# The second half of x loaded in 32-wide blocks and turned on VectorE; the third z group turned in the last block

## The chip, the cores and the metric

The kernel runs on one core of a Trainium2 chip. The metric is device time in microseconds (us) of one execution. The core has TensorE (matrix products into PSUM), VectorE (DVE in the profile), ScalarE (ACT), GpSimd (POOL) and SyncE (SP). SP, ScalarE and GpSimd can issue DMAs, each in the order of its own queue; all of them run on the core's 16 DMA engines.

## The reference

One inference step of a decoder layer with width 2048, for 256 prompt tokens and 32 sample tokens (8 sequences of 4), 288 tokens in all:

```
x = x + 1/2 * post1(SwiGLU_1(pre1(x)))      # RMSNorm before and after; inner width 5632
x = x + post2(HybridMixer(pre2(x)))         # GLA heads and HGRN2 heads, two recurrences
x = x + 1/2 * post3(SwiGLU_2(pre3(x)))

swiglu(x) = (silu(x @ w_gate) * (x @ w_up)) @ w_out
rmsnorm(x, g) = x * rsqrt(mean(x * x) + 1e-6) * g
```

The outputs are x for the prompt and for the sample tokens and the new states of the recurrences. Everything is 32-bit floating point, and the layer's weights, about 360 MB, are read once from HBM.

## The kernel before

**Layout.** x is held feature-major: 16 tiles x[k] of 128 features by 288 tokens. In DRAM it is token-major, so each tile has to be turned on the way in, and the result turned back on the way out.

**Products in three parts.** To keep 32-bit precision each operand is split into a rounded high part and the rest. For x, `split_x` (or `split_to`, lines 251 to 257) makes xh on ScalarE (line 252, with the norm's gain) and then xl on VectorE (line 253), which needs xh. For the weights, `Weights.pieces` makes wh on ScalarE (line 95) and wl on VectorE (line 96). Each product is three matmuls: xh by wh, xl by wh, xh by wl (lines 520 to 522). The rows' factor from the norm (rt) is multiplied in after the product, so that the products of the first block can begin before the norm is known.

**Weights.** A unit is 512 KB: 1024 columns by 128 partitions, in the FFN two steps k of 512 columns. SP issues the loads (line 63; the first unit as two rows, line 72) into three buffers named raw; `W.ahead` splits units into four buffers of wh and wl. A unit's load waits until the split has freed its raw buffer.

**Blocks.** `block` (line 511) multiplies 16 tiles of x by a column block of 512, into four PSUM tiles f. In the order of the program step k does its 12 matmuls (four f by three parts); after each step the block's `tick(k)` is called. The last `tail` units are done f by f, each f followed by its evacuation `evac`; then the ticks of those steps. The first FFN is `gate_0`, `up_0`, then pairs of these with `out` blocks of the chunk before. The framework's scheduler takes the program's order as its priority and sets each engine's order by its own estimates; `tc.issue_after(i)` keeps what is inside it behind instruction i in that order. Engines wait for each other by semaphores only where data or a buffer asks for it.

**The start.** `load_x(j)` loads two tiles of x token-major (128 tokens by 256 features, and 32 sample tokens) on SP (lines 276 and 277), after a memset of the rest of the third part. Eight such buffers are held. `x_tile(k)` turns one tile: three TensorE transposes by the identity into PSUM (lines 305 and 306), the split from PSUM, and a copy to x[k], on ScalarE for odd k (line 310) and on VectorE for even k (line 312). `x_first` is called by the first block's tick (`PreNorm.tick0`), two tiles ahead: after step k for tile k + 2. The first two tiles are made before the block; warm-up matmuls (line 294) stand around them. GpSimd issues four small parameter loads into stage2 (lines 265 to 268), ScalarE the load of the gains (line 264) and of araw, 2048 pieces of 64 B of the mixer's weights (line 775).

**The end.** In the last `out` blocks, out2_9_0 to out2_9_3 with two chunks each, every evacuated tile y[k] is squared and summed, and ScalarE makes z = y times gain (line 680). The tiles of the first three blocks (o < 3) are turned back in blocks of 32 by 32 on VectorE (`turn32`, lines 625 and 627, into one buffer b32 and bs32), and after the fourth tile `move32` (lines 636 and 640) moves the 32-blocks to their places in zT and zS, 20 DMAs that alternate between GpSimd's and SP's queues. The last block's four tiles are transposed on TensorE. `finish` then computes the norm, adds z and x (line 725) by quarters s = 0 to 3 and stores.

Of the kernel before, what the change touches and what calls it, by code (L numbers as in the profile page):

```python
# [16 lines left out]
P = 128  # L17
# [107 lines left out]
def trunk_kernel(ctx, tc, x_prompt, x_sample, state_gla, state_hgrn, norm_gains, f1_in, f1_out, f2_in, f2_out,  # L125
# [109 lines left out]

    FIRST = 2
    AHEAD = 4
    UPDATED = 8
# [17 lines left out]
    def split_x(gi, k):  # L256
        return split_to((xh[k], xl[k]), x[k], gain(gi, k))

    first = ExitStack()
    ldp = first.enter_context(tc.tile_pool(name="ld", bufs=8, side="right"))  # L260
    stage = ldp.tile([96, P], F32, name="stage", bufs=1)
    stage2 = ldp.tile([P, P], F32, name="stage2", bufs=1)
    G.memset(stage2, 0.0)
    S.dma_start(stage, norm_gains.rearrange("o g (k p) -> (o g k) p", p=P))
    G.dma_start(stage2[0:4, :], gla_b.rearrange("o (k p) -> (o k) p", p=P))
    G.dma_start(stage2[4:12, :], hgrn_gamma.rearrange("o (k p) -> (o k) p", p=P))
    G.dma_start(stage2[12:14, :], gla_norm.rearrange("o (k p) -> (o k) p", p=P))
    G.dma_start(stage2[14:15, :], hgrn_norm)
    xins = []
# [18 lines left out]
    load_x(3)  # L288
    load_x(4)
    def warm(n):  # L290
# [8 lines left out]
    V.tensor_copy(prm[:, 0:96], tp[:, 0:96])  # L299

    def x_tile(k):
        xin, c = xins[k // 2], slice(k % 2 * P, (k % 2 + 1) * P)
        tp = auxtile(f"tp_x{k}")
        for t in range(2):
            PE.transpose(tp[:, t * P:(t + 1) * P], xin[:, t, c], ident)
        PE.transpose(tp[:, TP:TP + P], xin[:, 2, c], ident)
        ins = split_to((xh[k], xl[k]), tp[:, 0:T], gain(0, k))
        with tc.issue_after(ins[0]), tc.issue_after(ins[1]):
            if k % 2:
                S.activation(x[k], tp[:, 0:T], AF.Copy)  # L310
            else:
                V.tensor_copy(x[k], tp[:, 0:T])
        return ins

    unit = []

    def x_first(k):

        with tc.issue_after(product[0]) if k >= FIRST else ExitStack():
            ins = x_tile(k)  # L320
        if k < 4:
            if k % 2 == 0:
                unit.append(W.pieces(2))
            with tc.issue_after(ins[0]), tc.issue_after(ins[1]):
                ins = next(unit[-1])
        if k % 2 == 1:
            if k >= 3:
                with tc.issue_after(ins[0]), tc.issue_after(ins[1]):
                    W.ahead(1)
            W.fill()  # L330
            if k // 2 + 5 < KT // 2:
                load_x(k // 2 + 5)
        return ins
# [232 lines left out]
    def ffn(tag, gcol, gnext, pn, before, fill=None):  # L566
# [3 lines left out]
        with ExitStack() as pools:  # L570
# [42 lines left out]

            lasts, zs = [], []

# [40 lines left out]
            def do_out(c, n):  # L656
# [8 lines left out]
                for o in range(4):  # L665
                    def ev(f, ps):
# [5 lines left out]
                        if end:  # L672
# [18 lines left out]
                    k = 4 * (c - 4) + o  # L691
# [49 lines left out]
    def mixer(pn, border):  # L741
        with ExitStack() as mx:
# [687 lines left out]

    pn = PreNorm("pre1", x_first, FIRST, 11)
    pn.late.append(prm2)
# [44 lines left out]
```

## Time and profile before

| what | value |
|---|---|
| median of 3 runs | 2281.41 us (2281.22 to 2283.21) |
| profiled execution, its own time | 2280.79 us |
| its span in the profile | 2279.0 us |
| TensorE matmuls busy | 2264.1 us, 99% |
| VectorE, ScalarE, GpSimd busy | 62%, 45%, 5% |
| granted TensorE clock, mean | 0.999 |
| DMA | 382 MB, mean 168 GB/s |

How to read the lines shown below. A line of the timeline has the start in us from the start of the span, the duration in us, engine, source line, operation, output and input tiles, their shapes, how many instructions were merged, and in brackets how long the engine was idle before it and what released it. A line of a group has the number of instructions, busy time in us, mean time of one in ns, and idle time before them by releaser; where it gives three durations they are the least, the median and the greatest, in ns. SPq is SP's queue of DMA issues. In the DMA view q1 holds SP's transfers, q10 ScalarE's and q0 GpSimd's: packets, MB, and the time their packets took as a share of the 16 engines' time; its GB/s row gives 40 equal slices of the stretch asked for. Matmul durations in the rows overlap, as TensorE is pipelined: the distance from start to start is the pace.

### The profile page before, as it was taken

The page shows a single profiled execution, that of the slowest core. Times are in us where ns is not written, and L with a number is a line of the kernel's source. Part 1 is how long each engine was busy: PE and PEld are TensorE (multiplying, and loading weights), DVE is VectorE, ACT ScalarE, POOL GpSimd, SP SyncE. Part 2 cuts the span into 40 slices and gives each one's busy share as a digit, 9 for nine tenths or more (in the row PEclk, how much of TensorE's full clock was granted, in tenths as well). Part 3 has the DMA queues.
Part 4 walks back from the last instruction along what each step waited for, and adds up shares of the span by engine and source line. Part 5 has one row for each costly group of instructions (what it writes and reads, how often), then busy time and mean ns, then how long its engine had stood idle before and what let it go on. Part 6 is the DMA issues. An engine that isn't in the chain of part 4 may idle for free.

```text
span 2279.0 us, 42090 instructions
## 1 busy us (share of the span) xinstructions
PE 2264.1 (99%) x17164; PEld 2252.0 (99%) x17164; DVE 1420.8 (62%) x2375; ACT 1034.4 (45%) x1603; POOL 115.8 (5%) x204
## 2 busy tenths in 40 slices
PE   9999999999999999999999999999999999999998
PEld 9999999999999999999999999999999999999997
DVE  7545545554555468889889754954555455545546
ACT  6443333333334346556656654644333333333344
POOL 0000000000000002001000000260000000000003
PEclk9999999999999999999999999999999999999999
DMA  7555555555555545456465554475555555555555
GB/s 218 169 165 165 165 167 165 166 166 167 167 167 185 166 158 163 139 171 198 144 183 159 167 183 160 141 203 169 165 166 164 166 167 166 167 167 167 167 163 151
DMA packets 228801, 382.42 MB, mean 168 GB/s; under 512 B 24018, under 2 KB 63936, under 8 KB 228608
## 3 DMA queue, kind: packets, MB, share of 16 engines
q1 hardware_dynamic: 219088, 366.27, 50.7%
q0 software_dynamic: 7344, 13.29, 2.1%
q8 instruction: 134, 2.20, 0.4%
q10 hardware_dynamic: 2176, 0.18, 0.1%
q14 instruction: 59, 0.48, 0.1%
HBM read 363.75 MB, written 11.80 MB: 165 GB/s over the span
## 4 chain that ended last, share of the span: by engine, by line
PE 94%; DVE 3%; DMA 1%; ACT 1%; issue 0%; DVEq 0%; SPq 0%; ACTq 0%
PE gate L522 9%; PE gate L520 9%; PE gate L521 9%; PE up L522 8%; PE up L520 8%; PE up L521 8%; PE out L521 8%; PE out L522 8%; PE out L520 8%; PE hfq L520 2%; PE hfq L522 2%; PE mo L522 1%; PE mo L520 1%; PE mo L521 1%; PE hfq L521 1%; PE v L520 1%
## 5 line engine op out<-in xcount | busy, mean ns | idle before, releaser
L96 DVE TENSOR_TENSOR wl<-raw,wh 128x1024 fp32r<-128x1024 f32 (+1 forms) x674 | 821.6, 1219 | 621.0 <-ACT wh L95 619.1
L95 ACT ACTIVATE wh<-raw 128x1024 fp32r<-128x1024 f32 (+1 forms) x674 | 711.6, 1057 | 1017.6 <-PE gate L521 315.8
L522 PE MATMUL gate<-xh,wl 128*128 128x288 f32 x1660 | 489.0, 295 | 0.2 <-DVE wl L96 0.2
L520 PE MATMUL gate<-xh,wh 128*128 128x288 f32 x1660 | 488.9, 296 | 0.3 <-ACT wh L95 0.3
L521 PE MATMUL gate<-xl,wh 128*128 128x288 f32 x1660 | 485.5, 295 | 0.0
L522 PE MATMUL out<-hh,wl 128*128 128x288 f32 x1408 | 415.1, 295 | 0.9 <-DVE wl L96 0.9
L521 PE MATMUL out<-hl,wh 128*128 128x288 f32 x1408 | 415.7, 295 | 0.0
L522 PE MATMUL up<-xh,wl 128*128 128x288 f32 x1408 | 415.0, 295 | 0.0
L520 PE MATMUL up<-xh,wh 128*128 128x288 f32 x1408 | 414.8, 295 | 0.1
L521 PE MATMUL up<-xl,wh 128*128 128x288 f32 x1408 | 414.6, 294 | 0.0
L520 PE MATMUL out<-hh,wh 128*128 128x288 f32 x1408 | 413.7, 294 | 0.0
L522 PEld LDWEIGHTS gate<-xh,wl 128*128 128x128 f32 x1660 | 311.5, 188 | 0.6 <-DVE wl L96 0.6
L520 PEld LDWEIGHTS gate<-xh,wh 128*128 128x128 f32 x1660 | 310.9, 188 | 1.2 <-ACT wh L95 0.5
L521 PEld LDWEIGHTS gate<-xl,wh 128*128 128x128 f32 x1660 | 310.4, 188 | 0.2
L522 PEld LDWEIGHTS out<-hh,wl 128*128 128x128 f32 x1408 | 264.7, 188 | 1.1 <-DVE wl L96 1.1
L520 PEld LDWEIGHTS out<-hh,wh 128*128 128x128 f32 x1408 | 264.6, 188 | 0.0
L520 PEld LDWEIGHTS up<-xh,wh 128*128 128x128 f32 x1408 | 264.1, 188 | 0.5 <-ACT g L590 0.3
L521 PEld LDWEIGHTS out<-hl,wh 128*128 128x128 f32 x1408 | 264.4, 188 | 0.0
L521 PEld LDWEIGHTS up<-xl,wh 128*128 128x128 f32 x1408 | 264.2, 188 | 0.1
L522 PEld LDWEIGHTS up<-xh,wl 128*128 128x128 f32 x1408 | 264.2, 188 | 0.0
L671 DVE TENSOR_TENSOR y<-out,y 128x288 f32<-128x288 f32 x288 | 121.4, 452 | 98.9 <-PE out L522 95.9
L520 PE MATMUL hfq<-xh,wh 128*128 128x288 f32 x256 | 77.5, 303 | 0.0
(381 smaller groups left out, 2598.2 us busy)
## 6 DMA issues: line engine op xcount, KB each, us to landing
raw<-in_ffn_w_in_dram SPq DMA_DIRECT2D x351, 512.0 KB, 3.4
raw<-in_ffn_w_out_dram SPq DMA_DIRECT2D x176, 512.0 KB, 3.5
raw<-in_mix_w_in_dram SPq DMA_DIRECT2D x64, 512.0 KB, 3.7
raw<-in_mix_w_in_dram SPq DMA_DIRECT2D x96, 256.0 KB, 3.2
raw<-in_mix_w_out_dram SPq DMA_DIRECT2D x32, 512.0 KB, 3.7
out_dram<-s POOLq DMA_DIRECT2D x32, 256.0 KB, 3.5
s<-in_state_gla_dram SPq DMA_DIRECT2D x16, 256.0 KB, 4.2
s<-in_state_hgrn_dram SPq DMA_DIRECT2D x16, 256.0 KB, 3.6
```

The source lines that it names most:

```text
L95: i1 = self.nc.scalar.activation(h[:, c], raw[:, c], AF.Copy).ins
L96: i2 = self.nc.vector.tensor_tensor(l[:, c], raw[:, c], h[:, c].bitcast(F32), op=ALU.subtract).ins
L520: yield lambda: PE.matmul(dst, w[0][:, c:c + P], parts[0], start=start, stop=False)
L521: yield lambda: PE.matmul(dst, w[0][:, c:c + P], parts[1], start=False, stop=False)
L522: yield lambda: PE.matmul(dst, w[1][:, c:c + P], parts[0], start=False, stop=stop)
L671: V.tensor_tensor(y[k], ps, y[k], op=ALU.add)
```

## The change

- Tiles 0 to 7 of x are loaded and transposed as before. Tiles 8 to 15 (TURNED = 8) go into one tile `xb` with 32 partitions for each 32-wide column block b of a tile: for every tile and b one DMA of 32 x 8 x 32 from the prompt, and for every b one DMA with the sample tokens of all eight tiles; 36 DMAs on GpSimd's queue, each in pieces of 128 B. The four loads into stage2 now come behind them on that queue.
- `x_turn(k + 1)` is one VectorE transpose in blocks of 32 by 32 of 128 x 288 from xb into x[k + 1], ordered behind the low split of tile k. For k >= 8 `x_tile(k)` is only the split, now from x[k] in SBUF; three TensorE transposes and the copy out of PSUM go. The four load_x of tiles 8 to 15 go from SP.
- The third z group (o == 2): turns and moves are put in a list `waiting`, and the last block's ticks take one entry each from step 1 on.
- The load of araw on ScalarE is ordered behind the instruction that follows the first norm.

In the order that the scheduler made, the matmuls of gate_0 from step 10 on put several xh-by-wh products ahead of those that need xl, and the last unit is done step by step. On VectorE turn k + 1 stands behind xl k, except that turn 14 stands behind the low half of the last weight unit of gate_0. In the tail one large turn of the third group (128 x 256) is left between the last two low halves of weights, where there were one large turn, two small ones (128 x 32) and an addition; the other turns stand ahead of the two or behind them.

```diff
     FIRST = 2
+    TURNED = 8
...
-    ldp = first.enter_context(tc.tile_pool(name="ld", bufs=8, side="right"))
+    ldp = first.enter_context(tc.tile_pool(name="ld", bufs=4, side="right"))
...
-    G.dma_start(stage2[0:4, :], gla_b.rearrange("o (k p) -> (o k) p", p=P))
-    G.dma_start(stage2[4:12, :], hgrn_gamma.rearrange("o (k p) -> (o k) p", p=P))
-    G.dma_start(stage2[12:14, :], gla_norm.rearrange("o (k p) -> (o k) p", p=P))
-    G.dma_start(stage2[14:15, :], hgrn_norm)
...
     load_x(3)
-    load_x(4)
+    xb = ldp.tile([P, KT - TURNED, T // TS, TS], F32, name="xb", bufs=1)
+    for b in range(4):
+        G.dma_start(xb[b * TS:(b + 1) * TS, :, TP // TS, :],
+                    x_sample.rearrange("b t (k q c) -> (b t) k q c", q=4, c=TS)[:, TURNED:KT, b, :])
+    for k in range(TURNED, KT):
+        for b in range(4):
+            c = k * P + b * TS
+            G.dma_start(xb[b * TS:(b + 1) * TS, k - TURNED, 0:TP // TS, :],
+                        x_prompt[0, :, c:c + TS].rearrange("(n p) c -> p n c", p=TS))
+    G.dma_start(stage2[0:4, :], gla_b.rearrange("o (k p) -> (o k) p", p=P))
...
+    def x_turn(k, ins):
+        if TURNED <= k < KT:
+            with tc.issue_after(ins[1]):
+                V.transpose(x[k], xb[:, k - TURNED].rearrange("p n c -> p (n c)"))
+
     def x_tile(k):
+        if k >= TURNED:
+            ins = split_x(0, k)
+            x_turn(k + 1, ins)
+            return ins
...
+        x_turn(k + 1, ins)
         return ins
...
-            if k // 2 + 5 < KT // 2:
-                load_x(k // 2 + 5)
...
-                                if o < 3:
+                                if o < 2:
                                     turn32(z, f)
                                     if f == 3:
                                         move32(o, *zt, (G, nc.sync))
+                                elif o == 2:
+                                    waiting.append(lambda: turn32(z, f))
+                                    if f == 3:
+                                        waiting.append(lambda o=o: move32(o, *zt, (G, nc.sync)))
...
-                          tail=2 if end and o == 3 else 1, hold=end and o == 3)
+                          tail=2 if end and o == 3 else 1, hold=end and o == 3,
+                          tick=lambda k: waiting.pop(0)() if waiting and k else None)
...
-            S.dma_start(araw, mi[:, 2048:2064].rearrange("(k p) c -> p k c", p=P))
+            with tc.issue_after(pre1.behind[2]):
+                S.dma_start(araw, mi[:, 2048:2064].rearrange("(k p) c -> p k c", p=P))
```

More of the change, by code (lines that the diff above doesn't have):

```diff
@@ L288, in trunk_kernel @@
     load_x(3)
-    load_x(4)
+    xb = ldp.tile([P, KT - TURNED, T // TS, TS], F32, name="xb", bufs=1)
[8 more added lines that the diff above has]
+    G.dma_start(stage2[0:4, :], gla_b.rearrange("o (k p) -> (o k) p", p=P))
+    G.dma_start(stage2[4:12, :], hgrn_gamma.rearrange("o (k p) -> (o k) p", p=P))
+    G.dma_start(stage2[12:14, :], gla_norm.rearrange("o (k p) -> (o k) p", p=P))
+    G.dma_start(stage2[14:15, :], hgrn_norm)
     def warm(n):
@@ L612, in do_in @@
                 block(f"up{tag}_{c}", KT, xrhs, ev_up, tick=pn.tick1 if c == 0 else None)
-            lasts, zs = [], []
+            lasts, zs, waiting = [], [], []
             def last_pool():
@@ L1429, in __init__ @@
                              f"fill{gnext}", gains, gnext, some)
-    pn = PreNorm("pre1", x_first, FIRST, 11)
+    pn = pre1 = PreNorm("pre1", x_first, FIRST, 11)
     pn.late.append(prm2)
```

## The prediction

> **What bounds the kernel now.** I read the page first, then the chain of waits, then the first 40 us and the last 25 us, because the change moves instructions only there; between them the order of every engine stays as it is.
>
> ```profile
> span 2279.0 us, 42090 instructions
> ...
> PE 2264.1 (99%) x17164; PEld 2252.0 (99%) x17164; DVE 1420.8 (62%) x2375; ACT 1034.4 (45%) x1603; POOL 115.8 (5%) x204
> ...
> PE 94%; DVE 3%; DMA 1%; ACT 1%; issue 0%; DVEq 0%; SPq 0%; ACTq 0%
> ```
>
> TensorE is busy 99% and is 94% of the chain. So time is won only where a TensorE instruction or a TensorE wait goes, and lost only where TensorE newly waits. The timeline of TensorE in the first block, with the first matmul of the block after it:
>
> ```profile
> 20.69 0.29 PE L522 MATMUL gate<-xh,wl 128*128 128x288 f32 x1
> ...
> 21.07 0.38 PE L520 MATMUL gate<-xh,wh 128*128 128x288 f32 x1
> ...
> 21.28 0.29 PE L521 MATMUL gate<-xl,wh 128*128 128x288 f32 x1
> ...
> 21.41 0.29 PE L522 MATMUL gate<-xh,wl 128*128 128x288 f32 x1
> ...
> 22.98 0.38 PE L520 MATMUL gate<-xh,wh 128*128 128x288 f32 x1
> 23.19 0.30 PE L521 MATMUL gate<-xl,wh 128*128 128x288 f32 x1
> ...
> 34.50 0.38 PE L520 MATMUL gate<-xh,wh 128*128 128x288 f32 x1
> ...
> 37.99 0.29 PE L520 MATMUL up<-xh,wh 128*128 128x288 f32 x1
> ```
>
> Matmuls follow each other by 0.13 us (21.28 to 21.41). A step k of the block is 12 of them, 1.59 us. Where three transposes of an x tile stand between two steps, 20.69 to 21.28 is 0.59 us instead of 0.26: a tile turned on TensorE costs 0.33 us. A step with its tile is 1.91 us (21.07 to 22.98).
>
> **The change, part by part.**
>
> *Transposes off TensorE.* Tiles 8 to 15 lose three transposes each: 8 x 0.33 = 2.7 us less TensorE work. That is the ceiling of this part; what is left of it depends on who delivers the tiles now. The rows of the two splitting engines in the first 40 us, and VectorE's 32 x 32 turn of a 128 x 256 tile from later in the kernel:
>
> ```profile
> L96 DVE TENSOR_TENSOR wl<-raw,wh 128x1024 fp32r<-128x1024 f32 x9 | 11.0, 1225 | 4.6 <-ACT wh L95 4.6
> L95 ACT ACTIVATE wh<-raw 128x1024 fp32r<-128x1024 f32 x9 | 9.5, 1056 | 0.5 <-DMA raw<-in_ffn_w_in_dram 0.5
> L253 DVE SCALAR_TENSOR_TENSOR xl<-tp_x,prm,xh 128x288 fp32r<-128x288 f32 x16 | 8.2, 516 | 6.9 <-ACT xh L252 6.9
> L252 ACT ACTIVATE xh<-tp_x,prm 128x288 fp32r<-128x288 f32 x16 | 8.0, 500 | 13.6 <-PE tp_x L306 13.6
> ...
> L625 DVE STREAM_TRANSPOSE b<-x x16: 398/404/446, 1450.9 to 1523.3; 128x256 f32<-128x256 f32 x16
> ```
>
> The turn of 128 x 288 is taken at 0.404 x 288/256 = 0.45 us. It runs in VectorE's queue behind the low split of the tile before (xl k, then turn k+1). So a tile's way is turn, then ScalarE's xh, then VectorE's xl, each waiting for the one before, and VectorE stands still while xh is made. Back to back, instructions on VectorE and ScalarE overlap by 0.08 to 0.1 us, as the next rows show (21.38 + 1.23 against 22.52). For a pair of tiles with its weight unit VectorE needs: xl 0.43, turn 0.45, wait for xh 0.54, xl 0.43, turn 0.37, weight low half 1.14 = 3.36 us. TensorE without transposes needs 2 x 1.59 = 3.18. VectorE's chain therefore becomes the slower one by about 0.2 us a pair, and there is nothing in hand:
>
> ```profile
> 21.38 1.23 DVE L96 TENSOR_TENSOR wl<-raw,wh 128x1024 fp32r<-128x1024 f32 x1 [0.91 <-ACT wh L95]
> ...
> 22.52 0.51 DVE L253 SCALAR_TENSOR_TENSOR xl<-tp_x,prm,xh 128x288 fp32r<-128x288 f32 x1
> ```
>
> This xl (tile 8) ends at 23.03 and TensorE uses it at 23.19. Following the changed order by these durations: step 8 would begin at 22.98 - 2 x 0.33 = 22.3 but its xl is there at 22.6, a wait of 0.13; steps 10 and 12 wait 0.1 and 0.2. Before tile 14 the order has the last weight unit's low half ahead of the turn: that unit's wh ends at 31.4, wl at 32.6, the turn at 33.05, xh 14 at 33.6, while TensorE is free at 32.3, a wait of 1.3. Together 1.75 us of new waits. The last two steps took 3.49 us before (34.50 to 37.99) where 24 matmuls take 3.18; those 0.3 go, as the last unit is now done k by k. Net: -2.7 + 1.75 - 0.3 = -1.2 us. Bounds: -3.0 if VectorE keeps up, 0 if the waits are twice as long. Eight copies of x out of PSUM (four on VectorE, four on ScalarE) go beside it; four memsets of VectorE go ahead of the first matmul, where TensorE is at its warm-up matmuls.
>
> *The pieces of x on the POOL queue.* Four of eight x loads leave SP; 36 DMAs of 32 x 8 x 32 go on POOL, pieces of 128 B, and araw (pieces of 64 B, ScalarE's queue) moves behind the first rstd. The DMA views of 0 to 60 us, of 3 to 5.5 us and of the last 54 us, POOL's issues of the same shape there, and POOL's first issue:
>
> ```profile
> GB/s 0 147 217 324 342 367 339 339 262 368 298 337 363 299 153 35 306 8 280 70 72 288 0 224 126 51 306 220 225 277 216 183 232 212 198 277 72 261 89 250
> ...
> q1 hardware_dynamic: 7927, 12.70, 66.0%
> q10 hardware_dynamic: 2176, 0.18, 2.7%
> ...
> q10 hardware_dynamic: 2012, 0.14, 55.8%
> q1 hardware_dynamic: 339, 0.49, 53.4%
> ...
> q0 software_dynamic: 1152, 0.99, 11.6%
> ...
> L636 POOL DMA_DIRECT2D zT<-b x24: 585/590/595, 2231.7 to 2265.1; - x24
> ...
> 1.89 0.68 POOL L265 DMA_DIRECT2D stage<-in_gla_b_gate_dram  x1 [0.31 <-POOL stage L263]
> ```
>
> In the last 54 us POOL's queue took 11.6% x 54 = 6.3 us of all sixteen engines for 0.99 MB; a 32 KB DMA is 0.21 us. The 36 are 7.5 us. POOL issues one per 0.59 us, so while it issues (1.9 to 23 us) it takes 35% of the engines. Four x loads gone are 1.18 MB at 60 x 66%/12.70 = 3.1 us per MB, 3.7 us; araw 1.5 us (of 2.7% x 60 = 1.6). So 2.3 us more work, in the stretch where the engines are full (217 to 367 GB/s in slices of 1.5 us up to 20 us). What is late for it is the third weight unit. Up to it the queue carries three x loads, two rows of weights and two units, 2.46 MB, and araw's queue 0.18: by the GB/s row that is moved at 10.6 us. Without araw and with POOL's 35% from 2.9 us on (I take 1 us from issue to data), t = 10.6 - 1.5 + 0.35 (t - 2.9), t = 12.4 us. The fourth unit (behind three more x loads: 4.0 MB, moved at 14.9) was used at 16.25, so 1.3 us go from there to its use: 13.7 us.
>
> ```profile
> 6.27 0.63 ACT L95 ACTIVATE wh<-raw 128x512 fp32r<-128x512 f32 x1 [0.44 <-DMA raw<-in_ffn_w_in_dram]
> ...
> 11.95 1.57 ACT L95 ACTIVATE wh<-raw 128x512 fp32r<-128x512 f32 x2
> ...
> 14.70 0.51 DVE L253 SCALAR_TENSOR_TENSOR xl<-tp_x,prm,xh 128x288 fp32r<-128x288 f32 x1
> ...
> 15.51 0.30 PE L521 MATMUL gate<-xl,wh 128*128 128x288 f32 x1
> ...
> 16.25 1.06 ACT L95 ACTIVATE wh<-raw 128x1024 fp32r<-128x1024 f32 x1 [0.17 <-DMA raw<-in_ffn_w_in_dram]
> ```
>
> Before, ScalarE began that unit at 12.5 (the second of the two at 11.95), without a wait. At 13.7 it is 1.2 later; xl 4 stands behind its low half on VectorE, ended at 15.21 and was used at 15.51, so 0.3 is in hand and TensorE is 0.9 us late. The very first row of weights (used at 6.27 after a wait of 0.44) no longer shares with araw, about -0.3 as ScalarE's xh 0 then holds it up; but that head start is lost again at this wait. So +0.9. Bounds: -0.3 (nothing late) to +4.
>
> In the row of 3 to 5.5 us araw took as much of the engines as the weights for a third of the bytes. The Trainium skill ("DMA: Bandwidth & Descriptors", Queues, rings and completion order) says that an engine goes round its queues packet by packet, not byte by byte; the trace agrees with 55.8% against 53.4%, and this speaks against the change: by that rule a POOL queue that never ran empty would hold half of the engines, which is the second rival below.
>
> *Late loads with cover.* The four small parameter loads go out at 23 us instead of 1.9 and are used after the first rstd, in the block after; araw is used in the mixer. Both cost nothing.
>
> *The tail.* Rows of VectorE, ScalarE, TensorE, SP and POOL:
>
> ```profile
> 2256.99 1.23 DVE L96 TENSOR_TENSOR wl<-raw,wh 128x1024 fp32r<-128x1024 f32 x1 [1.62 <-ACT wh L95]
> ...
> 2258.60 0.43 DVE L625 STREAM_TRANSPOSE b<-z 128x256 f32<-128x256 f32 x1
> ...
> 2259.05 1.18 DVE L96 TENSOR_TENSOR wl<-raw,wh 128x1024 fp32r<-128x1024 f32 x1
> ...
> 2257.30 1.06 ACT L95 ACTIVATE wh<-raw 128x1024 fp32r<-128x1024 f32 x1
> ...
> 2260.29 0.40 PE L522 MATMUL out<-hh,wl 128*128 128x288 f32 x1 [0.90 <-DVE wl L96]
> ...
> 2259.06 5.19 SPq L636 DMA_DIRECT2D zT<-b  x8
> ...
> 2265.64 0.56 POOL L640 DMA_DIRECT2D zS<-bs  x1
> ...
> 2269.70 2.72 DVE L725 SCALAR_TENSOR_TENSOR o<-zT,rc,xT 128x512 f32<-128x512 f32 x4
> ```
>
> TensorE waits 0.9 us at the last weight unit because VectorE puts turns of z's third group between the last two low halves. In the changed order one turn is left between them: first low half to 2258.13, one turn to 2258.49, wh there at 2258.36, so the last low half starts at 2258.5 instead of 2259.05: -0.55 us. The last turn ends 1.1 us later and so does the start of that group's moves (SP 2259.06, POOL to 2266.2). They would be issued by 2267.3 and, at some 2 us more, landed by 2269.4; the sum that reads them comes third of four from 2269.70, at 2271.1, less 0.55. Cover remains: 0 cost. Bounds: -0.9 to +0.6 (the shift less what is won).
>
> **Sum.** -1.2 + 0.9 - 0.55 = -0.85 us on the profiled execution, whose span is 2279.0 and whose own time is 2280.79, 0.6 under the median of 2281.41 of the runs shown. Forecast: 2280.6.
>
> **Rivals.**
> - *VectorE keeps up and no weights are late.* For it: VectorE and ScalarE are never told to wait for TensorE on these tiles, so they may run ahead. Against it: xl 8 had 0.16 us in hand. All three gains: -3.0 - 0.3 - 0.55 = -3.85 at the most, 2277.6.
> - *The small pieces push the weights back further (slower).* The place is the third weight unit. Were POOL's queue always filled, with araw's share 55.8/(55.8 + 53.4) = 51%, t = 9.1 + 0.51 (t - 2.9) = 15.6: 3.2 us later than forecast, 2283.8. It takes pieces 1.5 times as dear as those of the last 54 us. From 58% of the engines on (t = 17.8, pieces 1.7 times as dear) the loss passes 0.2%. For it: these pieces come from HBM, those were within SBUF. Against: araw's 64 B pieces, from HBM, cost 2.7% x 960 us/2176 = 12 ns each, and 0.21 us x 16/256 is 13.
> - *POOL issues too slowly (slower).* Tile 15's last piece is the 36th; its turn is due at 34 us. Over 0.8 us per issue the turns wait. At twice 0.59 the last is issued at 44 and the block ends some 13 us late: 2294. Against it: 585 to 595 ns, while VectorE turned and split.
>  The Trainium skill ("SBUF — State Buffer", SBUF: two separate sides) warns that VectorE's fp32 copies within SBUF lock POOL out of writing descriptors; by that rule copies would slow these issues, but the x copies here come from PSUM, and no row shows a slowed issue.
> - *Nothing moves*: the parts cancel; this is inside the first case.
>
> **How the numbers follow.** Likeliest case, 2279.3 to 2282.2: 0.56. VectorE keeps up, 2277.6 to 2279.3: 0.14. Weights later, 2282.2 to 2286: 0.18, and beyond 2286: 0.08. POOL too slow: 0.04. A measurement of this kernel can tell about 0.2%, 4.6 us, from no change. The first three cases lie within it but for a sliver; slower 0.12, faster 0.02, same 0.86. The range, 2277.9 to 2284.6, leaves out less than 2 in 10, most of it above.
>
> **What would show it.** Right: matmul steps of 1.59 us from step 7 on with a wait of about a microsecond before tile 14 and `up` beginning near 37.6; third weight unit's wh at 13.7; 36 POOL issues 0.59 apart; the last TensorE wait down to 0.4. Wrong: wh rows waiting several microseconds for raw in the first 20 us, VectorE waiting for xb, or `o` waiting for zT at the end.

## The result, and the profile after

| | kernel before | changed kernel |
|---|---|---|
| time, median (lowest to highest) | 2281.22 us (2279.49 to 2283.72) | 2285.99 us (2284.99 to 2288.00) |
| ratio to before, 95% interval | | 1.0022 [1.0015, 1.0029] |
| profiled execution: own time, span | 2280.79, 2279.0 us | 2286.11, 2284.1 us |

The change makes the kernel about 4.8 us slower, where 0.8 us faster was forecast. The page of the changed kernel, its first lines and the chain:

```profile
span 2284.1 us, 42087 instructions
...
PE 2264.4 (99%) x17140; PEld 2250.2 (99%) x17140; DVE 1419.7 (62%) x2375; ACT 1033.0 (45%) x1599; POOL 136.2 (6%) x240
...
PE 93%; DVE 2%; DMA 2%; ACT 1%; issue 1%; POOL 0%; DVEq 0%; SPq 0%; ACTq 0%; POOLq 0%
```

TensorE has 24 matmuls less and is busy as long as before: what the transposes gave is spent again. To see where, I set every matmul of the changed kernel against the same matmul of the kernel before. The changed kernel's TensorE is 1.44 us late when the first block pair ends, 2.55 late after a wait near 725 us, 1.94 late at 2200 us (the profile of before has a wait of 0.9 us of its own at 885 us), and 5.12 late at the last block's end. Behind that nothing more is lost: the span is 5.1 us longer. So there are three places: start, 725 us, end.

The start, in the timelines of ScalarE, TensorE and VectorE (start, duration, engine, line, and in brackets the idle time before it and what ended it):

```profile
14.27 1.06 ACT L95 ACTIVATE wh<-raw 128x1024 fp32r<-128x1024 f32 x1 [1.86 <-DMA raw<-in_ffn_w_in_dram]
17.86 1.06 ACT L95 ACTIVATE wh<-raw 128x1024 fp32r<-128x1024 f32 x1 [1.45 <-DMA raw<-in_ffn_w_in_dram]
...
16.07 0.40 PE L540 MATMUL gate<-xh,wh 128*128 128x288 f32 x1 [0.46 <-ACT xh L253]
17.07 0.40 PE L541 MATMUL gate<-xl,wh 128*128 128x288 f32 x1 [0.60 <-DVE xl L254]
35.58 0.40 PE L540 MATMUL gate<-xh,wh 128*128 128x288 f32 x1 [1.16 <-ACT xh L253]
38.88 0.29 PE L540 MATMUL up<-xh,wh 128*128 128x288 f32 x1
58.58 0.72 PE L414 MATMUL pre<-acc,onesD 128*128 128x288 f32 x2 [0.20 <-DVE acc L388]
...
57.98 0.45 DVE L388 TENSOR_TENSOR acc<-acc,sq 128x288 f32<-128x288 f32 x1
```

The third weight unit (14.27) waited 1.86 us for its data; TensorE is 1.56 us late at step 4 (17.07 against 15.51). Steps 8 to 13 take 3.37 us a pair where 24 matmuls take 3.18. Tile 14 (35.58) comes 1.46 us after the matmul before it, instead of 0.13. `up` begins at 38.88 instead of 37.99. The matmul of the first rstd (`pre`) then waits for the last sum of squares, which ended at 58.43. Before the change that matmul ran at 57.07 without a wait, and the last sum had ended at 56.0. The squares start behind the gate's evictions on ScalarE. The rows of before, and then ScalarE's of the changed kernel:

```profile
57.07 0.40 PE L394 MATMUL pre<-acc,onesD 128*128 128x288 f32 x1
...
54.43 1.57 DVE L368 TENSOR_TENSOR acc<-acc,sq 128x288 f32<-128x288 f32 x3
...
36.46 0.71 ACT L590 ACTIVATE g<-gate 128x288 f32<-128x288 f32 x2
...
38.01 0.72 ACT L590 ACTIVATE g<-gate 128x288 f32<-128x288 f32 x2
...
39.54 0.46 ACT L364 ACTIVATE acc<-x 128x288 f32<-128x288 f32 x1
```

```profile
38.84 1.29 ACT L610 ACTIVATE g<-gate 128x288 f32<-128x288 f32 x4
...
40.95 0.46 ACT L384 ACTIVATE acc<-x 128x288 f32<-128x288 f32 x1
```

The end, first POOL's first moves of z and VectorE's turn of z's second group before the change:

```profile
2231.68 1.17 POOL L636 DMA_DIRECT2D zT<-b  x2 [696.13 <-DVE bs L627]
...
2241.56 0.45 DVE L625 STREAM_TRANSPOSE b<-z 128x256 f32<-128x256 f32 x1 [0.54 <-DMA zT<-b]
```

Then the changed kernel, in the timelines of POOL, VectorE, ScalarE and TensorE, and the stretches around the waits:

```profile
2233.63 0.59 POOL L656 DMA_DIRECT2D zT<-b  x1 [695.69 <-DVE bs L647]
2235.58 0.58 POOL L656 DMA_DIRECT2D zT<-b  x1 [1.36 <-issue]
...
2246.67 0.45 DVE L645 STREAM_TRANSPOSE b<-z 128x256 f32<-128x256 f32 x1 [3.70 <-DMA raw<-in_ffn_w_out_dram]
...
2259.33 1.06 ACT L95 ACTIVATE wh<-raw 128x1024 fp32r<-128x1024 f32 x1 [3.93 <-DMA raw<-in_ffn_w_out_dram]
...
2262.48 0.40 PE L542 MATMUL out<-hh,wl 128*128 128x288 f32 x1 [1.51 <-DVE wl L96]
2263.95 0.61 PE L542 MATMUL out<-hh,wl 128*128 128x288 f32 x1 [0.40 <-DVE wl L96]
...
core 0: us, PE busy (x) PEld busy (x) DVE busy (x) ACT busy (x) POOL busy (x), PEclk, DMA share, GB/s
2260.40:2263.80 3.40, 1.59 (x8) 1.13 (x8) 3.11 (x6) 1.36 (x2) 0.00 (x0) 1.00 0.00 0
2263.90:2267.20 3.30, 3.25 (x13) 3.26 (x14) 1.45 (x5) 0.87 (x2) 2.57 (x5) 0.50 0.32 49
```

POOL issues its first move of z and then stands still for 1.36 us, with nothing that the profile shows to wait for. Its last moves of z's first group land at 2246.3 and 2246.6 instead of 2241.5 and 2242.9. VectorE's turn of the second group needs them landed: it starts at 2246.67, before it was 2241.56 behind a wait of 0.54 us; of these 5.1 us 1.9 are TensorE's lateness. (The row names a weight load; it waits for several transfers.) The second group's moves, the last two weight loads behind them on SP's queue and the last low halves follow late. TensorE waits for these, and behind the waits its granted clock is 0.50 for 3.4 us: matmuls follow each other by 0.24 us instead of 0.13. The waits, less the 0.9 us that was there before, make 1.7 us and the slow stretch 1.45, together 3.2.

### The profile page after: what moved, and what is told of

Same layout as the page of the kernel before. It is cut to its first block, busy times and chain, and to the rows that moved or that the text cites. A ratio compares the mean times of both kernels' runs of the same rounds, so it can differ in the third digit from the quotient of the medians.

```text
span 2284.1 us, 42087 instructions
## 1 busy us (share of the span) xinstructions
PE 2264.4 (99%) x17140; PEld 2250.2 (99%) x17140; DVE 1419.7 (62%) x2375; ACT 1033.0 (45%) x1599; POOL 136.2 (6%) x240
## 4 chain that ended last, share of the span: by engine, by line
PE 93%; DVE 2%; DMA 2%; ACT 1%; issue 1%; POOL 0%; DVEq 0%; SPq 0%; ACTq 0%; POOLq 0%
PE gate L542 9%; PE gate L540 9%; PE gate L541 9%; PE out L541 8%; PE out L542 8%; PE out L540 8%; PE up L542 8%; PE up L540 8%; PE up L541 8%; PE hfq L540 2%; PE hfq L542 2%; PE mo L542 1%; PE mo L540 1%; PE mo L541 1%; PE hfq L541 1%; ACT wh L95 1%
```

## The experiments

"Over before" is the difference of the medians on the same chip; the next columns are read from TensorE of one profiled execution each, against the profile of before: lateness at 115 us, what a wait near 725 us added, whether POOL stood still in z's first group, and what the end (from 2200 us to the last block's end) added. The one profile of before has a wait of 0.9 us at 885 us that most others lack, and the profiles come from several chips. So the three columns together differ from "over before" by up to 1.8 us, and differences of a few tenths in them say little.

| kernel | over before, us | ratio, interval | start | 725 | POOL's stop | end |
|---|---|---|---|---|---|---|
| changed | +4.8 | 1.0022 [1.0015, 1.0029] | +1.4 | 1.1 | yes | +3.2 |
| changed again, another chip | +6.2 | 1.0029 [1.0018, 1.0041] | +2.9 | 0.9 | yes | +1.2 |
| changed, end undone | +6.0 | 1.0030 [1.0018, 1.0041] | +2.5 | 1.3 | yes | +2.0 |
| before, end alone | -1.0 | 0.9996 [0.9987, 1.0004] | -0.1 | 0 | no | -0.3 |
| before, araw alone | -0.3 | 0.9998 [0.9989, 1.0007] | -0.4 | 0 | no | +0.1 |
| changed, 1 KB runs | +3.1 | 1.0011 [1.0002, 1.0020] | +0.9 | 0.8 | 3rd group | +0.6, and 1.2 behind the last block |
| changed, 24 small matmuls | +12.4 | 1.0051 [1.0037, 1.0065] | +8.6 | 0 | yes | +2.4 |
| changed, 53 memsets on POOL | +5.2 | 1.0024 [1.0015, 1.0033] | +2.9 | 1.1 | yes | +2.8 |
| changed, turn 14 first | +4.7 | 1.0020 [1.0012, 1.0029] | +0.6 | 0.7 | yes | +1.6 |
| turn 14 first, rstd later | +5.3 | 1.0021 [1.0012, 1.0029] | +1.3 | 1.0 | yes | +2.0 |
| changed, 8 more loads | +4.4 | 1.0020 [1.0011, 1.0028] | +2.2 | 1.2 | no | +0.2 |
| before, 36 more loads | +4.5 | 1.0019 [1.0010, 1.0027] | +0.4 | 0 | yes | +3.2 |
| four tiles, loads later | +1.2 | 1.0005 [0.9996, 1.0014] | +0.9 | 0 | 2nd group | -0.6 |
| four tiles, rstd later | +2.2 | 1.0009 [1.0000, 1.0018] | -0.8 | 0 | 2nd group | +2.9 |
| changed, three repairs | +2.2 | 1.0010 [1.0001, 1.0019] | +0.3 | 1.0 | no | +0.3 |
| four tiles, repairs | -0.2 | 0.9999 [0.9991, 1.0008] | -1.0 | 0 | no | -1.0 |
| before, 24 matmuls less | -1.2 | 0.9996 [0.9987, 1.0004] | -1.6 | 0.3 | no | -0.4 |

**Which part costs.** The end of the change undone, the end alone, and araw alone:

```diff
-                                if o < 2:
+                                if o < 3:
...
-                                elif o == 2:
-                                    waiting.append(lambda: turn32(z, f))
```

> The changed kernel with the start as changed, but z's third group turned and moved in the evictions again, as before the change. Theory A, the loss at the end comes from the moved turns: the end then takes what it took before (last TensorE wait about 1.2 us, no stretch at half clock), only the start's +1.6 to +2.0 us stays, and the time is about 1.8 us above the kernel before. Theory B, the loss at the end comes from something ahead of the moved turns (the turns of z's second group came 3.1 us later against TensorE already, behind moves of the first group that landed late after POOL had stood still for 1.36 us): the loss at the end stays at about 3 us, the last TensorE wait is near 1.8 us and is followed by some 3.4 us at half clock, and the time is 4 to 5 us above the kernel before.

> The kernel before with only z's third group turned and moved in the last block's steps. Theory A, the moved turns cost the end: the last TensorE wait grows to about 1.8 us, a stretch at half clock follows, and the time is about 3 us above the kernel before. Theory B, they are harmless or win the forecast 0.55 us, and the end is lost by what comes ahead of them: the last TensorE wait falls from 1.2 us to 0.6 or so, and the time is 0 to 0.6 us below the kernel before.

> The kernel before with only the load of araw moved behind the first rstd. Forecast of the prediction's step: the first row of weights some 0.3 us earlier, the third weight unit no later than 12.5 us, the first rstd between 0.3 us earlier and unchanged, time within 0.5 us of the kernel before. Rival, the moved load costs something where it now stands (it is issued on ScalarE's queue between the first rstd and the first gated evictions, and the products after it wait): the step to the first rstd is as before, but from there on TensorE is 0.6 us or more later, as it was in the changed kernel between the first matmul of up (+0.9) and the first rstd (+1.5).

Theory B holds in the main: without the moved turns the end still loses 2.0 us, in three waits of 0.7 to 1.0 us and without the stretch at half clock that was expected, and the moved turns by themselves lose nothing. TensorE's last wait, 0.90 us in the row of before that the prediction shows, in the kernel with the end alone:

```profile
2258.55 0.40 PE L522 MATMUL out<-hh,wl 128*128 128x288 f32 x1 [0.40 <-DVE wl L96]
```

That 0.5 us of wait is what was forecast, but that the moved turns win it is not shown: the end of this profile is only 0.3 us shorter, and in the last run below, with the end as before, the same wait is 0.49 us. Most of what this profile gains comes ahead of the end (TensorE is 1.5 us early at 2200 us), and the interval of the time contains no change.

araw's move behaves as forecast: the start is 0.36 us earlier and the time the same within the interval. So the loss at the end is made by something in the changed start.

**The pieces.** The same loads with 1 KB runs, its turn of tile 14 placed ahead of the last low half by the order of instructions (which the expectation did not foresee):

```diff
-            c = k * P + b * TS
+            c = (k - TURNED) * TP
...
-                        x_prompt[0, :, c:c + TS].rearrange("(n p) c -> p n c", p=TS))
+                        x_prompt[0, 2 * b * TS:(2 * b + 1) * TS, c:c + TP])
```

> The changed kernel with the same 32 loads of x for the last eight tiles in number, order, queue, bytes and destination, but each reads 32 stretches of 1 KB where the changed kernel reads 256 pieces of 128 B; the values are other elements of x, so the output is not the reference's. Theory A, the short pieces slow the engines (about 4.9 us of all sixteen in the changed kernel, and the rest of the traffic beside them): POOL's waits for landings shrink from about 6 us to under 2, the third weight unit is split at about 13 us instead of 14.3, up begins at 37 to 38 instead of 38.9, and the time is 1 to 2 us below the changed kernel. Theory B, it is the bytes and the POOL queue as such: third unit at 14 or later, up at 38.9, time as the changed kernel's.

```profile
14.24 1.06 ACT L95 ACTIVATE wh<-raw 128x1024 fp32r<-128x1024 f32 x1 [1.38 <-DMA raw<-in_ffn_w_in_dram]
```

The third unit is as late as with short pieces (14.24 against 14.27), so their length alone is not what delays it. They do cost something: in the first 60 us the 36 loads took 8.2% of the engines with pieces of 128 B and 7.2% with 1 KB, and SP's queue 3.6 against 3.2 us of all engines for each MB (3.1 before the change):

```profile
q1 hardware_dynamic: 6518, 11.25, 67.1%
q0 software_dynamic: 1280, 1.19, 8.2%
```

```profile
q1 hardware_dynamic: 6673, 11.57, 61.8%
q0 software_dynamic: 1280, 1.19, 7.2%
```

The first fence is the changed kernel's DMA view, the second that of the 1 KB runs (packets, MB, share). The Trainium skill ("DMA: Bandwidth & Descriptors", Why small descriptors are slow) says that short pieces from HBM are dear; the direction agrees, but it is not the cause of the late unit. `up` begins 0.16 us before that of the kernel before here, which the next run assigns to the place of turn 14.

**The order on VectorE, and the sum of squares.** Turn 14 ahead of the last low half, and then the first rstd one step later as well:

```diff
-                with tc.issue_after(ins[0]), tc.issue_after(ins[1]):
+                with tc.issue_after(ins[0]), tc.issue_after(ins[1]), tc.issue_after((turned or ins)[-1]):
                     W.ahead(1)
...
-    pn = pre1 = PreNorm("pre1", x_first, FIRST, 11)
+    pn = pre1 = PreNorm("pre1", x_first, FIRST, 12)
```

> The changed kernel with the turn of tile 14 put ahead of the last weight unit's low half on VectorE; nothing else is moved. By the prediction's step the wait of TensorE before tile 14 (1.46 us) falls to 0.2 to 0.4, the weight unit's low half comes 0.5 us later and is still in time, and up begins about 1 us earlier. Whether this reaches the end is disputed: if the first rstd waits for the sum of the squares (theory Q: its instructions on ScalarE and VectorE stand behind the weight units, so TensorE's earlier start only waits longer there), the first rstd comes less than 0.5 us earlier; if not, the whole 1 us stays.

> The changed kernel with tile 14's turn first, and with the first rstd's matmul one step of the block later (step 12 instead of 11). Theory Q, that matmul waits for the sum of squares, which ended 1.06 us ahead of it before the change and 0.15 us ahead of it, with TensorE waiting, in all five profiles with the changed start: the wait of 0.5 to 1.3 us there goes, the matmul runs 20.7 us after the first matmul of up, and TensorE is at +0.1 to +0.4 us against the kernel before after it, where it was at +0.8. Rival, something else holds it up, the waits for weights in that block: the wait moves along to step 12 and TensorE stays at +0.8. The end is not touched, so the time is 2 to 5 us above the kernel before.

The matmuls of `up` and `pre` with the turn first, then `pre` of the second kernel:

```profile
38.05 0.29 PE L542 MATMUL up<-xh,wh 128*128 128x288 f32 x1
...
57.77 0.72 PE L416 MATMUL pre<-acc,onesD 128*128 128x288 f32 x2 [0.23 <-DVE acc L390]
```

```profile
59.89 0.65 PE L416 MATMUL pre<-acc,onesD 128*128 128x288 f32 x2
```

The wait of 1.46 us goes and `up` begins 0.8 us earlier than in the changed kernel. `pre` comes 0.8 us earlier too (57.77 against 58.58), so by the sign written for that run theory Q would be refuted; but `pre` still waits for the sum, and what it loses differs from profile to profile, so this run alone does not decide. One step later it no longer waits: TensorE's lateness grows by 0.3 us between `up` (+0.96 in that run, whose third unit was later) and 115 us, and not by 0.6; this rest falls at `up`'s first products, not at `pre`. With four tiles turned, below, the step takes a wait of 0.9 us away. That is what theory Q says: the squares begin behind the gate's evictions, of which four instead of two now come after the gate's last matmul, and their chain had 1.07 us in hand (56.00 to 57.07).

**Fewer tiles, loads later.** Four tiles turned, POOL's 20 loads behind the copy of tile 2 (two more x loads stay on SP's queue):

```diff
-    TURNED = 8
+    TURNED = 12
...
+        go = G.tensor_copy(gate[:, 0:1], x[2][:, 0:1]).ins
+        es.enter_context(tc.issue_after(go))
```

> The changed kernel with four tiles turned instead of eight (12 to 15; tiles 8 to 11 are loaded in rows and turned by TensorE as before the change), and POOL's 20 loads of them start only once tile 2 has been copied. If the pieces' traffic in the first 12 us is what makes the third weight unit late, its split is back at 12 to 12.6 us and TensorE loses nothing at step 4; up then begins between 0.9 us earlier and 0.3 us later than before the change (four tiles save 1.3 us, tile 14 waits about 1.3). If the third unit is late for another reason (the order of SP's queue without the later x loads, or araw), it stays at 14 us or so. The time is not disputed here: 0 to 4 us above the kernel before, by how the end falls out.

```profile
13.07 1.06 ACT L95 ACTIVATE wh<-raw 128x1024 fp32r<-128x1024 f32 x1 [0.89 <-DMA raw<-in_ffn_w_in_dram]
...
58.03 0.48 PE L425 MATMUL pre<-acc,onesD 128*128 128x288 f32 x1 [0.91 <-DVE acc L399]
```

The third unit is 1.2 us earlier: two thirds of its lateness (12.5 to 14.27) go when POOL's traffic of the first 12 us goes. What in that traffic delays it, and the rest, I did not settle.

**What stops POOL.** First, where instructions stand: 24 matmuls of 8 columns on TensorE, 53 memsets on POOL.

```diff
+    for _ in range(24):
+        PE.matmul(ps[:, 0:8], onesD, onesD[:, 0:8], start=True, stop=True)
```

```diff
+    for _ in range(53):
+        G.memset(pad, 0.0)
```

> The changed kernel with 24 matmuls of 8 columns put behind the warm-up, into a tile that nothing reads, so that TensorE has as many instructions ahead of the later blocks as before the change. Theory T, the loss at the end (and the 1 us near 725 us) comes from where TensorE's own instruction loads of 16 KB (about 1 us each on one DMA engine, one per 17 us) now fall among the weight loads: then they fall as before, the stall near 725 us and the one at the end go, and the time is at most 2 us above the kernel before, plus what the 24 matmuls cost at the start (0.5 to 2 us). Theory P, it comes from POOL, which stands still 1.36 us at its second move of z: nothing changes at the end, last TensorE wait near 1.8 us or spread over several waits, time 5 us or more above the kernel before.

> The changed kernel with 53 one-column memsets on POOL behind its loads, so that POOL's later instructions stand where they stood, counted in blocks of 128 (36 loads taken as two instructions each and three waits were added; the stalls of about 1 us came 62 to 66 rows apart in the kernels so far). Theory P, the loss at the end comes from POOL's stall at its second move of z's first group: the 1.36 us stall goes from there, z's second group is turned about 2241.6 us plus the start's delay, the last TensorE wait is back to about 1.2 us or below, and the time is 1.5 to 2.5 us above the kernel before. Theory T, the loss comes from TensorE's instruction loads: the end is as slow as in the changed kernel, time about 5 us above the kernel before, with or without the stall of POOL.

Neither helps the end: POOL stops at the same move (1.36 and 1.66 us). So the count of POOL's instructions is not what places the stop. The first run is not the test of theory T that was meant: each of its 24 matmuls shows as two instructions in the trace, so TensorE has 17,188, 24 more than before the change and not as many. Only the wait near 725 us went with them. Counted in pieces by the shapes of its loads and moves, POOL's long stops without a shown cause stand behind 15,038 and 27,966 in the kernel before (256 pieces for a move of `b`, 128 for one of `bs`), where they fall into the moves of x and TensorE does not wait:

```profile
1460.67 0.58 POOL L636 DMA_DIRECT2D xT<-b  x1 [1.14 <-issue]
1517.47 0.56 POOL L640 DMA_DIRECT2D xS<-bs  x1 [1.20 <-issue]
```

In the changed kernel, which has moved 9,216 pieces more by then, they stand behind 28,606 and 42,174: the second is its second move of z. With four tiles it is 41,022, in z's second group. With 1 KB runs (as many loads, but 7,168 pieces fewer) it is 40,766, in z's third group; there the last norm, whose squares POOL copies behind its moves, waits 1.2 us behind the last block:

```profile
2265.70 0.58 POOL L656 DMA_DIRECT2D zT<-b  x1 [1.18 <-issue]
...
2271.10 0.62 PE L395 MATMUL postf<-onesD,sq 128*128 128x1 f32 x4 [1.19 <-POOL sq L744]
```

Two runs test the count alone: 8 more loads in the changed kernel, and 36 more, with 9,216 pieces, in the kernel before.

```diff
         V.tensor_copy(prm[:, 96:111], tp[:, 0:15])
+        for i in range(8):
+            G.dma_start(spare, x_prompt[0, :, 0:TS].rearrange("(n p) c -> p n c", p=P))
```

> The changed kernel with 8 more loads on POOL's queue behind the first rstd (256 pieces of 128 B each, into a small tile that nothing reads). Counted in pieces of POOL's loads and moves, POOL stood still for 0.9 to 1.7 us behind 28,606 and 42,174 pieces in the changed kernel and in the one with 53 memsets, behind 15,038 and 27,966 in the kernel before (40,382 in all), and behind 41,022 in the kernel with four tiles turned; in the changed kernel the second of these is its second move of z. Theory D, the count decides: 2,048 pieces more put that stall into the moves of x near 1530 us, z's moves have none, z's second group is turned without the 3 us of delay, no stretch at half clock, and the time is 3 us or more below the changed kernel, that is 1 to 2 us above the kernel before. Rival: the stall is where z's moves begin, whatever came before (or the loss at the end has another cause): end and time as in the changed kernel, about 5 us above the kernel before.

> The kernel before with 36 more loads on POOL's queue behind the first rstd, 256 pieces of 128 B each, into a tile that nothing reads; the start, TensorE's instructions and the turns of z are as before. POOL has then moved as many pieces when z's moves begin (41,918) as in the changed kernel. Theory D, the count of pieces decides: POOL stands still for about 1.4 us at its second move of z, z's second group is turned some 3 us later against TensorE, the last TensorE wait grows by 1 us or more, with a stretch at half clock or without, and the time is 1.5 to 4 us above the kernel before. Rival, the loss at the end needs the change itself (later start, fewer TensorE instructions): no stall there, time within 0.5 us of the kernel before.

POOL and VectorE in the changed kernel with 8 more loads:

```profile
1535.42 1.16 POOL L659 DMA_DIRECT2D xT<-b  x2 [1.65 <-issue]
...
2233.92 1.17 POOL L659 DMA_DIRECT2D zT<-b  x2 [693.94 <-DVE bs L650]
...
2243.50 0.45 DVE L648 STREAM_TRANSPOSE b<-z 128x256 f32<-128x256 f32 x1 [0.23 <-issue]
```

and in the kernel before with 36 more, with its stretch at half clock:

```profile
2232.54 0.58 POOL L639 DMA_DIRECT2D zT<-b  x1 [1.36 <-issue]
...
2243.58 0.45 DVE L628 STREAM_TRANSPOSE b<-z 128x256 f32<-128x256 f32 x1 [3.64 <-DMA raw<-in_ffn_w_out_dram]
...
2261.00:2264.00 3.00, 3.00 (x13) 3.00 (x14) 0.92 (x2) 0.87 (x2) 3.00 (x7) 0.50 0.69 94
```

Eight loads put the stop into the moves of x and the end's loss goes (+3.2 to +0.2); 36 loads that nothing reads put it into the unchanged kernel's moves of z and make the loss (+3.2), with the same 1.36 us and nearly the same wait (3.64 against 3.70 us). This kernel has all of TensorE's instructions and the turns of before, so the loss at the end needs neither theory T nor the moved turns. In all eight profiles with the stop in z's first group the end adds 1.2 to 3.2 us; in the six where the end has no stop it adds -1.0 to +0.3. That the count of pieces decides where POOL stops, within some 1,800 pieces, is shown by this; why POOL stops there is not. Yet the time with 8 more loads is +4.4 where 1 to 2 was expected, since I had priced the start by one profile (+1.4; the five with that start have 1.4 to 2.9, 2.4 in the mean) and left out the wait near 725 us. So what the stop costs is read from the profiles and from the 36 loads' +4.5; the times of the changed kernel with and without the 8 loads, taken on different chips, do not tell it.

**Four tiles, rstd later, and all repairs.** The three repairs of the changed kernel are turn 14 first, the rstd one step later, and 8 more loads on POOL to move its stop. With four tiles they are the loads later, the rstd one step later and 24 more loads; turn 14 stays where it was:

> The kernel with four tiles turned and POOL's loads begun after tile 2, with the first rstd's matmul one step later. By theory Q TensorE's wait of 1.2 us there goes and TensorE is at -0.2 to 0 us against the kernel before behind it; with z's third group turned in the last block's steps (-0.6 us at the end in this kernel without the later step) the time is 0.3 to 1 us below the kernel before, not below the kernel with the change of the end alone. If the wait only moves along, it is 0.5 to 1.5 us above the kernel before.

> The changed kernel as it is, a second time. If the first profile is typical: POOL stands still 1.36 us at its second move of z, the turn of z's second group waits 3 to 4 us, and the time is 4 to 6 us above the kernel before; the start's share at the first rstd is between 1.5 and 3.0 us. If the stall is an accident of the first profile, it is not there and the time is still as high, by the start.

> The changed kernel with three repairs at once: tile 14's turn first, the first rstd's matmul one step later, 8 more loads on POOL's queue. By the sums from the single runs: at the start 2.4 - 1.1 - 0.5 = +0.8 us (0.3 to 1.5), near 725 us +1.0, at the end 0 to -0.5; the time is 1 to 2.5 us above the kernel before and 2 to 4 us below the changed kernel on the same chip. If the end's loss is not in most executions, or the start costs what it costs by the loads alone, the gain over the changed kernel is under 1.5 us.

> The kernel with four tiles turned, POOL's loads begun after tile 2 and the first rstd one step later, with 24 more loads on POOL's queue behind the first rstd (43,454 pieces when z's moves begin, so that the stall behind about 41,000 to 42,200 pieces falls ahead of them). By the single runs: start -0.8 to 0, no wait near 725 us, end -0.5: 0.5 to 1.5 us below the kernel before, as the kernel with the change of the end alone. If the 1.9 us wait at the end and the half clock behind it, which that kernel showed without the 24 loads, come again, the stall behind the count is not their cause, and the time is 2 us above the kernel before.

On one chip: changed kernel +6.2 us, with the three repairs +2.2. The 4.0 us gained lie within what the profiles give: start 2.6 (2.9 to 0.3), end 0.9 to 2.9 (1.2 or 3.2 to 0.3). With four tiles, the rstd later lost its gain at the end, to a wait of 1.63 us and half clock behind it. The stop of 1.06 us in z's second group stands ahead of that wait. But four tiles with the loads later, without the later rstd, had the same stop (1.05 us) and an end 0.6 us shorter than the kernel before, so a stop there does not always cost. With 24 loads more the stop falls into the moves of x (0.65 us, behind 42,558 pieces) and TensorE doesn't wait at the end, but the time is still that of the kernel before; its profile is of the fastest of its 11 executions. No version of the start beats the kernel before by more than can be told, nor does the change of the end alone.

**The wait near 725 us.** It stands in the ninth `out` block of the first FFN, behind a weight load that landed 5.4 us after its issue instead of 3.4:

```profile
728.88 0.40 PE L540 MATMUL out<-hh,wh 128*128 128x288 f32 x1 [0.88 <-DVE u L618]
```

The last run leaves 24 matmuls of the first gate block out of the kernel before:

```diff
+                if name == "gate1_0" and f < 3 and 4 <= k < 12:
+                    three.pop(1)
```

> The kernel before with 24 matmuls of the first gate block left out (the low half of x times the high half of the weights, steps 4 to 11, three of four column blocks), so the output is not quite the reference's; POOL, the loads and the end are as before. Theory T, the wait of about 1 us near 725 us comes with 24 fewer TensorE instructions, by where its instruction loads of 16 KB fall among the weight loads: it is there, 0.7 to 1.3 us. Rival, it comes from the later start: it is not there. The first block is shorter by at most 24 x 0.13 = 3.2 us; less, where its weights come no sooner. The end shows neither stall of POOL nor half clock.

TensorE loses 0.3 us there, and the load takes 4.1 us. All nine profiles of kernels with 8 turned tiles and 24 instructions less on TensorE have the wait, with 0.7 to 1.3 us; it went with the 48 instructions of the small matmuls, and no kernel with four turned tiles has it. Theory T is neither shown nor refuted; the cause of this 1 us stays open.

## Why the prediction was wrong

- *Transposes off TensorE*, forecast -1.2 by `up`: the mechanism is right, the gain smaller. VectorE's chain is the slower one, 3.6 us a pair where 3.36 was forecast. The waits of steps 8 to 13, forecast 0.45, make 0.6 us, and the wait before tile 14 was to be 1.3 and is 1.33 beyond the pace. From step 5 (18.89 against 17.23) to `up` (38.88 against 37.99) TensorE wins 0.8 us.
- *The pieces on POOL's queue*, forecast +0.9: mis-sized. Third unit at 14.27 instead of 13.7, TensorE +1.56 at step 4. The loads took less of the engines than forecast (4.9 us instead of 7.5), while SP's own traffic was dearer, 3.6 instead of 3.1 us per MB, a term that was not in the sum. That this term is what was missing is not shown: with 1 KB runs it falls to 3.2 and the third unit is as late. "36 POOL issues 0.59 apart" failed too: from the tenth on they wait for landings of earlier loads and end at 28.7 us instead of 23; this cost nothing, as no turn waited:

```profile
11.28 1.16 POOL L295 DMA_DIRECT2D xb<-in_x_prompt_dram  x2 [1.49 <-DMA xb<-in_x_prompt_dram]
```

- *What the start hands on.* The working stopped at `up` and carried its number to the end. It booked the last unit done k by k as -0.3 and missed that the gate's evictions, and the squares behind them, then come later. Between `up` and 115 us 0.5 to 1.3 us are lost, 0.3 at `up`'s first products and the rest at `pre`. Together the start was to be -0.3 and is +1.4 (2.4 in the mean).
- *The tail*, forecast -0.55: with the end alone the last wait is down to 0.4 as written, and the end 0.3 shorter. "Cover remains: 0 cost" for z's third group holds: in no profile does a sum `o` wait for zT, and in the changed kernel's nothing is lost behind the last block. The step that failed lies ahead of it, and in this profile it is the largest error: the moves of z's first and second group were taken as unchanged, a term put at nothing without a reason. POOL's stop makes it +3.2 (1.2 when the changed kernel is profiled again, where the start's +2.9 is larger). POOL's stops of 1.1 and 1.2 us stood in the profile of before, in the moves of x; the working asked of the 36 new loads only what they cost where they are issued, not what they shift on their queue 2200 us later.
- The rival with later weights had the right sign and the right place in the start, with a time (2283.8) below the measured one; the wait near 725 us, the end and the half clock behind a wait were in no rival.

## What to carry to other kernels

A transfer that is moved onto a queue can also move what happens on that queue by count, as it did here on POOL's, 2200 us later; look through the whole trace for stalls of that queue that cost nothing today, and ask where they fall after the change. Follow a late or early block to the next place where something has less than the shift in hand (here the sum of squares, 1.07 us), not only to its own end. And price a change from several profiles where its parts are of a microsecond: the same start cost 1.4 to 2.9 us.

## What the runs showed of the hardware that was not expected

- POOL's DMA issue stops for about 0.8 to 1.7 us at places set by the count of pieces that it has issued (15,038, then 27,454 to 28,606, then 40,766 to 42,174 here); 53 other instructions in between change nothing. At other places the profile shows shorter stops, 0.65 us behind 42,558 pieces for one.
- TensorE's granted clock fell to 0.50 for 3.4 us after a stretch of 3.4 us in which it was busy for 1.59. The Trainium skill ("TensorE: Matmul & The Clock Gate", The HAM clock gate) gives 3.4 us as the window and speaks of an idle one; the length agrees, but a window half busy was enough here, and similar waits in other runs (1.61 and 0.39 us with turn 14 first and the rstd later) left the clock at 1.00.
- 24 matmuls of 8 columns, 48 instructions in the trace, took from 6.9 to 14.5 us. The clock fell to 0.50 while they ran, at 9.8 us, though TensorE was busy without a gap, and stood there for 10.2 us; half of these, 5.1 us, is lost of the 8.6 us at that kernel's start. The first 27 instructions, nearly all at full clock, then all 48, and the stretch at half clock:

```profile
6.89 3.28 PE L360 MATMUL pad<-onesD 128*128 128x8 f32 x27
...
L360 PE MATMUL pad<-onesD x48: 248/256/363, 6.9 to 14.3; 128*128 128x8 f32 x48
...
10.00:20.00 10.00, 10.00 (x45) 9.98 (x46) 1.06 (x3) 1.02 (x2) 6.69 (x12) 0.50 0.80 189
```
